# A 3×3 convolution with 2×2 max pooling: five row differences change engine, and the order of the head is rewritten

## The chip, the cores and the metric

The kernel runs on one core of a Trainium2 chip. The metric is the device time of one execution in microseconds (us), and where a kernel was run several times, the median. Engines are named as in the profile: PE is TensorE (PEld its weight loads), DVE is VectorE, ACT is ScalarE, POOL is GpSimd, and SP is SyncE, which here only issues DMA transfers.

## The reference

`x` has shape (16, 64, 64, 64), `weight` (128, 64, 3, 3), both float32. Each image is convolved with padding 1, and the maximum over 2×2 blocks is taken:

```python
conv[b, co] += weight[co, ci, kh, kw] * x_pad[b, ci, kh:kh+h, kw:kw+w]   # over ci, kh, kw
output[b, c, i, j] = np.max(conv[b, c, 2*i:2*i+2, 2*j:2*j+2])
```

The output has shape (16, 128, 32, 32).

## The kernel before

**Tiling.** Two images lie on the 128 partitions (two times 64 channels). The eight pairs of images are worked on as four groups `j`, each with one pair of the kind "k" and one of the kind "w". A pair is cut into four chunks `q` of 16 rows, which give 8 rows of pooled output. One chunk of a k pair and the same chunk of the w pair make a step `i` = 4j + q, so there are 16 steps.

**Arithmetic.** The two conv rows that a pooled row needs share input rows, so the kernel forms products with sums and differences of weight rows. For a k pair the weights alone are combined, and the rows of `x` go in as they are, plus the row sum `ks`. For a w pair the rows of `x` are combined as well, into four tiles: `ws` (sum of the two rows, step WS), `we` (their difference, step E), `wz` and `wy` (differences with the rows above and below, steps Z and Y). These read float32 rows from `wx` and write bfloat16 tiles for TensorE. `ks` reads and writes bfloat16. All of them pass through one function, `row_op` (line 248).

**Steps on TensorE** (`taps`, line 183): each group is six matmuls, three column taps for each of the two images. Step i has PA (two groups: 12 matmuls), PB (two), PR (uses KS) for the k pair, and P2 (uses E), P0 (uses Z), P3 (uses Y), P1 (uses WS) for the w pair: nine groups. A name such as PB.5 means PB of step 5.

**Accumulators.** There are four PSUM tiles `acc`, handed out from a queue `free` in the order in which the program text gives them back. PA and PB each take one for the k pair, P2 and SE (the seed, ScalarE) each one for the w pair.

**Steps that empty them.** EV (k) and ev (w) copy the first accumulator to SBUF on ScalarE (line 286) and free it. MX and mx take the maximum of the second accumulator and that copy on VectorE (line 299). PR.i adds after MX.i, and P1.i after mx.i. OD and od copy the odd columns on ScalarE (line 304), and CM and cm take the column maximum on VectorE (line 318), free the second accumulator and issue the output's DMA on SP. After CM.i the rows `wx` of step i + 4 are loaded, also on SP. SE.i writes minus the first accumulator to the second on ScalarE (line 295), ahead of P0.i.

**Order.** Nothing is reordered by the compiler: every engine works its queue in the order in which the program emits it. This order is written out by hand in three strings: `HEAD` (the weights, and steps 0 to 3), `STEADY` (run for i = 4 to 12, each name with an offset to i) and `TAIL`. `XO` and `XE` cast the first chunk of the first k pair on VectorE, X1 and X2 the second chunk on ScalarE, and the rest of that pair is loaded by `kload`, a DMA issued on POOL's queue that converts to bfloat16.

**VectorE and GpSimd.** Each GpSimd row operation waits for the last SBUF row operation that was emitted for VectorE ahead of it (`on_gpsimd`, `behind`): in `STEADY`, E, Z and Y of step i + 1 wait for WS.i. Before the change E.0, all KS and all WS are on VectorE, and E.1 to E.15, all Z and all Y on GpSimd. In the old `HEAD` some KS and WS come between E, Z and Y of a step. `kload` of the rest of the first pair is issued behind Y.0.

Of the kernel before, what the change touches and what calls it, by code (L numbers as in the profile page):

```python
# [11 lines left out]
def kernel(  # L12
# [21 lines left out]
    nc = tc.nc  # L34
# [4 lines left out]
    SUB = mybir.AluOpType.subtract  # L39

    B, CI, H, W = x.shape
# [28 lines left out]
    def behind(inst, other):  # L70
        if other is not None:
            tc.add_manual_dep(inst.ins, other.ins.name, SYNC, reason="order")

    def on_vector(inst):
        sbuf_op[0] = inst
        return inst

    def on_gpsimd(inst):
        behind(inst, sbuf_op[0])
        return inst  # L80


    def rows_of(p, lo, hi):
        return x[2 * p : 2 * p + 2].rearrange("b c h w -> (b c) h w")[:, lo:hi, :]

    def chunk(q):
        return (2 * R * q + (q > 0), min(H, 2 * R * (q + 1) + 1))
# [4 lines left out]
    def kload(j, lo, hi):  # L92
        if j not in kx:
            kx[j] = kx_pool.tile([128, H, W], BF16, name="kx")
        return nc.gpsimd.dma_start(out=kx[j][:, lo:hi, :], in_=rows_of(2 * j, lo, hi))  # L95
# [138 lines left out]
    def row_out(name, i):  # L234
        j, q = divmod(i, NQ)
        if (name, j) not in row:
            row[name, j] = row_pool.tile([128, HO, W], BF16, name=name)
        return row[name, j][:, q * R : (q + 1) * R, :]

    def row_in(t, first, pad):  # L240
        a = first + pad
        return t[:, a : a + 2 * R - 1 : 2, :]

    def row_op(engine, name, i, a, b, op):
        j, q = divmod(i, NQ)
        t, pad = (kx[j], 0) if name == "ks" else (wx[j % 2], 1)
        f = 2 * R * q
        return engine.tensor_tensor(  # L248
            out=row_out(name, i), in0=row_in(t, f + a, pad), in1=row_in(t, f + b, pad), op=op
        )  # L250
# [5 lines left out]
        on_vector(row_op(nc.vector, "ws", i, 0, 1, ADD))  # L256

    def we(i):
        if i == 0:
            on_vector(row_op(nc.vector, "we", i, 1, 0, SUB))  # L260
        else:
            on_gpsimd(row_op(nc.gpsimd, "we", i, 1, 0, SUB))

# [3 lines left out]
    def wy(i):  # L267
        on_gpsimd(row_op(nc.gpsimd, "wy", i, 2, 0, SUB))
        j, q = divmod(i, NQ)
        if i == 0:  # L270
            kload(0, chunk(2)[0], H)
        if q == 1 and j + 1 < NP // 2:
            kload(j + 1, 0, H // 2 + 1)
        if q == 2 and j + 1 < NP // 2:
            kload(j + 1, H // 2 + 1, H)


    ev, od, ot = {}, {}, {}
# [64 lines left out]
    def cast_more(first):  # L343
# [18 lines left out]
        "X2": lambda: cast_more(1),  # L362
        "PA": pa, "PB": pb, "PR": pr, "P0": p0, "P1": p1, "P2": p2, "P3": p3,
        "KS": ks, "WS": ws, "E": we, "Z": wz, "Y": wy, "SE": seed,
        "EV": lambda i, h=None: evac(("k", i), h), "ev": lambda i, h=None: evac(("w", i), h),
        "MX": lambda i, h=None: rowmax(("k", i), h), "mx": lambda i, h=None: rowmax(("w", i), h),
# [3 lines left out]
    for m in BLOCKS:  # L370
# [2 lines left out]

    HEAD = """
        D2 g0 D0 g2 GS g1 TD2 VD2 TG0 VG0 XO TD0 VD0 TG2 VG2 TG1 VG1 XE GM PA.0 GP TGM VGM TGP
        KS.0 E.0 WS.0 PB.0 EV.0 X1 Z.0 Y.0 VGP P2.0 MX.0 SE.0 X2 PA.1 EV.1 PR.0 P0.0 P3.0 E.1 P2.1 KS.1
        OD.0 CM.0 PB.1 Z.1 ev.0 WS.2 SE.1 P0.1 ev.1 mx.0 P1.0 od.0 Y.1 P3.1 MX.1 PR.1 OD.1 PA.2
        E.2 WS.1 KS.2 cm.0 PB.2 CM.1 P2.2 Z.2 mx.1 P1.1 EV.2 MX.2 PR.2 SE.2 od.1 cm.1 OD.2 CM.2
        Y.2 E.3 Z.3 Y.3 P0.2 P3.2 KS.3 WS.3 PA.3 E.4 ev.2 mx.2 P2.3 EV.3 Z.4 PB.3 SE.3 Y.4 MX.3
        P1.2 od.2 cm.2 P0.3 P3.3 ev.3 PR.3 KS.4 WS.4  # L380
    """
    STEADY = """
        PA+0 OD-1 E+1 CM-1 P2+0 mx-1 EV+0 Z+1 PB+0 SE+0 Y+1 P1-1 MX+0 P0+0 od-1 P3+0 cm-1 ev+0
# [63 lines left out]
```

## Time and profile before

| | us |
|---|---|
| median of 6 runs | 109.58 |
| lowest and highest | 108.97 and 110.64 |
| the profiled execution's own time | 110.64 |
| its span, first to last instruction | 108.8 |
| busy: PE, DVE, ACT, POOL | 100.7, 83.5, 72.9, 64.9 |

The profiled execution is the slowest of the six. The span leaves out what lies ahead of the first and behind the last instruction, here 1.8 us. A line of a timeline reads: start, duration (both us), engine, source line, operation, output and inputs with partitions × elements and type, and how many instructions are merged. In brackets stands the idle time ahead of it and what ended that. A line of the chain of waits reads: start, duration, engine, tile and source line. [...]

### The profile page before, as it was taken

How to read it: one execution, taken by the hardware profiler on the slowest of the kernel's cores; microseconds unless marked ns; L12 is line 12 of the kernel's file. 1: busy time of each engine (PE TensorE's matmuls, PEld its weight loads, DVE VectorE, ACT ScalarE, POOL GpSimd, SP SyncE). 2: the span in 40 equal slices, each digit the busy share in tenths (PEclk: the TensorE clock that was granted, in tenths of full speed). 3: DMA queues.
4: the chain of work that ended last, by engine and by line, in shares of the span. 5: the costliest groups of instructions: out<-in, count | busy, mean ns of one | idle time of the engine just before them, and what ended most of it. 6: DMA issues, size and time to landing. Idle time of an engine off the chain costs nothing.

```text
span 108.8 us, 2348 instructions
## 1 busy us (share of the span) xinstructions
PE 100.7 (93%) x900; PEld 52.1 (48%) x900; DVE 83.5 (77%) x109; ACT 72.9 (67%) x92; POOL 64.9 (60%) x73
## 2 busy tenths in 40 slices
PE   5999879999999999999999999999999999999820
PEld 2564434544545555555555555555555555545400
DVE  0494779996989786868797869688787888685950
ACT  4565966549666767676877876776867676776820
POOL 6200997699696969490869594943967444445000
PEclk9999999999999999999999999999999999999985
DMA  3999469999995979999974889999939422223052
GB/s 73 355 325 353 169 76 225 272 240 217 185 343 206 220 115 198 312 195 349 289 243 132 179 115 267 243 257 335 279 146 216 158 101 99 96 96 102 0 193 96
DMA packets 12475, 21.96 MB, mean 202 GB/s; under 512 B 944, under 2 KB 9136, under 8 KB 12464
## 3 DMA queue, kind: packets, MB, share of 16 engines
q1 hardware_dynamic: 11312, 18.03, 49.9%
q0 software_dynamic: 1008, 3.65, 22.8%
q8 instruction: 7, 0.11, 0.5%
q10 hardware_dynamic: 144, 0.13, 0.3%
q14 instruction: 4, 0.03, 0.1%
HBM read 17.07 MB, written 8.39 MB: 234 GB/s over the span
## 4 chain that ended last, share of the span: by engine, by line
PE 69%; DVE 14%; DMA 7%; issue 4%; ACT 2%; SPq 0%; DVEq 0%; ACTq 0%
PE acc L183 67%; DVE acc L299 9%; DMA ksecond<-in_x_dram 7%; DVE ws L248 2%; DVE o L318 2%; PE acc L135 2%; ACT od L304 2%; ACT kx L344 1%; DVE ks L248 0%; SPq L100 0%; DVE zeros L112 0%; DVEq L299 0%; ACTq L304 0%
## 5 line engine op out<-in xcount | busy, mean ns | idle before, releaser
L183 PEld LDWEIGHTS <-wt 64*128 64x128 bf16 x864 | 48.5, 94 | 47.6 <-issue 4.2
L299 DVE TENSOR_TENSOR acc<-acc,ev 128x1024 f32<-128x1024 f32 (+1 forms) x34 | 39.3, 1164 | 10.1 <-PE acc L183 9.4
L183 PE MATMUL acc<-kx,wt 64*128 64x504 bf16 (+3 forms) x384 | 46.6, 373 | 0.5 <-ACT kx L344 0.4
L286 ACT COPY ev<-acc 128x1024 f32<-128x1024 f32 (+1 forms) x34 | 32.6, 964 | 12.8 <-PE acc L183 11.2
L248 POOL TENSOR_TENSOR we<-wx 128x512 bf16<-128x512 f32 x15 | 19.1, 1273 | 17.3 <-DVE ws L248 9.3
L304 ACT COPY od<-acc 128x512 f32<-128x512 f32 x32 | 18.8, 587 | 11.3 <-PE acc L183 11.2
L318 DVE TENSOR_TENSOR o<-acc,od 128x512 f32<-128x512 f32 x32 | 21.8, 689 | 5.5 <-ACT od L304 5.5
L248 POOL TENSOR_TENSOR wz<-wx 128x512 bf16<-128x512 f32 x16 | 20.3, 1271 | 8.6 <-DVE ws L248 7.7
L248 POOL TENSOR_TENSOR wy<-wx 128x512 bf16<-128x512 f32 x16 | 20.3, 1270 | 5.6 <-DVE ws L248 5.6
L295 ACT ACTIVATE acc<-acc 128x1024 f32<-128x1024 f32 x16 | 16.1, 1008 | 2.6 <-PE acc L183 2.2
L183 PE MATMUL acc<-we,wt 64*128 64x504 bf16 (+1 forms) x96 | 13.3, 377 | 0.8 <-POOL we L248 0.5
L183 PE MATMUL acc<-ws,wt 64*128 64x504 bf16 (+1 forms) x96 | 13.3, 377 | 0.6 <-DVE acc L299 0.4
L183 PE MATMUL acc<-ks,wt 64*128 64x504 bf16 (+1 forms) x96 | 13.3, 377 | 0.2
L183 PE MATMUL acc<-wy,wt 64*128 64x504 bf16 (+1 forms) x96 | 13.3, 377 | 0.0
L183 PE MATMUL acc<-wz,wt 64*128 64x504 bf16 (+1 forms) x96 | 13.3, 377 | 0.0
L248 DVE TENSOR_TENSOR ws<-wx 128x512 bf16<-128x512 f32 x16 | 13.1, 821 | 0.0
L248 DVE TENSOR_TENSOR ks<-kx 128x512 bf16<-128x512 bf16 x16 | 8.9, 559 | 0.6 <-ACT kx L344 0.6
L135 PE MATMUL acc<-zeros 128*128 128x512 bf16 x8 | 3.6, 631 | 1.2 <-DVE zeros L112 1.2
L95 POOL DMA_DIRECT2D kx<-in_x_dram x7 | 4.1, 588 | 0.0
L148 PEld LDWEIGHTS <-wq 128*128 128x128 bf16 x28 | 2.6, 134 | 1.0 <-issue 0.6
L148 PE MATMUL acc<-ident,wq 128*128 128x128 bf16 x28 | 2.8, 281 | 0.0
L350 DVE TENSOR_TENSOR wq<-wraw 128x192 bf16<-128x192 f32 x1 | 0.5, 501 | 2.5 <-DMA wraw<-in_weight_dram 2.5
(26 smaller groups left out, 15.1 us busy)
## 6 DMA issues: line engine op xcount, KB each, us to landing
out_dram<-o SPq DMA_DIRECT2D x31, 256.0 KB, 4.3
wx<-in_x_dram SPq DMA_DIRECT2D x8, 512.0 KB, 7.4
wx<-in_x_dram SPq DMA_DIRECT2D x4, 544.0 KB, 8.8
kx<-in_x_dram POOLq DMA_DIRECT2D x4, 496.0 KB, 9.2
wx<-in_x_dram SPq DMA_DIRECT2D x4, 480.0 KB, 5.0
kx<-in_x_dram POOLq DMA_DIRECT2D x3, 528.0 KB, 8.9
kfirst<-in_x_dram SPq DMA_DIRECT2D x1, 544.0 KB, 4.2
ksecond<-in_x_dram SPq DMA_DIRECT2D x1, 512.0 KB, 7.4
```

What stands on the lines that cost most here:

```text
L95: return nc.gpsimd.dma_start(out=kx[j][:, lo:hi, :], in_=rows_of(2 * j, lo, hi))
L135: return nc.tensor.matmul(acc[t][:, h], zeros[:, 0:128], zeros, start=True, stop=True, skip_group_check=True)
L148: nc.tensor.transpose(tp[:, (j - lo) * 128 : (j - lo + 1) * 128], wq[:, j : j + 2, :].rearrange("a b c -> a (b c)"), ident,)
L183: nc.tensor.matmul(dst[:, half, i0:i1, o0:o1], wt[lo : lo + CI, m0 + kw - half, :], rows(lo, i0, i1, c0, c1), start=start and kw == 1, sto ...
L248: return engine.tensor_tensor(out=row_out(name, i), in0=row_in(t, f + a, pad), in1=row_in(t, f + b, pad), op=op)
L286: nc.scalar.copy(out=ev[g][:, halves(h)], in_=acc[ta[g]][:, halves(h)])
L295: nc.scalar.mul(acc[t], acc[ta["w", i]], -1.0)
L299: nc.vector.tensor_tensor(out=t, in0=t, in1=ev[g][:, halves(h)], op=MAX)
L304: nc.scalar.copy(out=od[g][:, halves(h)], in_=acc[tb[g]][:, halves(h), :, 1::2])
L318: nc.vector.tensor_tensor(out=o, in0=acc[tb[g]][:, s, :, 0::2], in1=od[g][:, s], op=MAX)
L344: nc.scalar.copy(out=kx[0][:, klo2 + first : khi2 : 2, :], in_=ksecond[:, first::2, :])
L350: "D2": lambda: on_vector(nc.vector.tensor_sub(out=slots(D2), in0=g2, in1=g1)),
```

## The change

Three things are changed.

1. E.1 to E.4 are computed on VectorE, where E.0 already was. E.5 to E.15 stay on GpSimd.
2. The load of the rest of the first k pair is issued on POOL's queue behind E.0, ahead of Z.0. Before, it was issued behind Y.0.
3. `HEAD` is reordered. In steps 1 to 4 WS, KS and E of a step stand together ahead of Z and Y, so that both GpSimd operations wait for the last of the three. Z.4 and Y.4, which stood ahead of KS.4 and WS.4, now stand behind them. The order of TensorE's groups, of the emptying steps and of the accumulators handed out changes somewhat. `STEADY` and `TAIL` are the same.

```diff
     def we(i):
-        if i == 0:
-            on_vector(row_op(nc.vector, "we", i, 1, 0, SUB))
+        if i < 5:
+            inst = on_vector(row_op(nc.vector, "we", i, 1, 0, SUB))
+            if i == 0:
+                behind(kload(0, chunk(2)[0], H), inst)
         else:
             on_gpsimd(row_op(nc.gpsimd, "we", i, 1, 0, SUB))
...
         j, q = divmod(i, NQ)
-        if i == 0:
-            kload(0, chunk(2)[0], H)
         if q == 1 and j + 1 < NP // 2:
...
-        KS.0 E.0 WS.0 PB.0 EV.0 X1 Z.0 Y.0 VGP P2.0 MX.0 SE.0 X2 PA.1 EV.1 PR.0 P0.0 P3.0 E.1 P2.1 KS.1
-        OD.0 CM.0 PB.1 Z.1 ev.0 WS.2 SE.1 P0.1 ev.1 mx.0 P1.0 od.0 Y.1 P3.1 MX.1 PR.1 OD.1 PA.2
-        E.2 WS.1 KS.2 cm.0 PB.2 CM.1 P2.2 Z.2 mx.1 P1.1 EV.2 MX.2 PR.2 SE.2 od.1 cm.1 OD.2 CM.2
-        Y.2 E.3 Z.3 Y.3 P0.2 P3.2 KS.3 WS.3 PA.3 E.4 ev.2 mx.2 P2.3 EV.3 Z.4 PB.3 SE.3 Y.4 MX.3
-        P1.2 od.2 cm.2 P0.3 P3.3 ev.3 PR.3 KS.4 WS.4
+        KS.0 E.0 WS.0 PB.0 EV.0 X1 Z.0 Y.0 VGP P2.0 MX.0 SE.0 X2 PA.1 EV.1 WS.1 KS.1 E.1 PR.0
+        P0.0 P3.0 Z.1 Y.1 OD.0 CM.0 P2.1 ev.0 PB.1 SE.1 mx.0 P0.1 P1.0 MX.1 P3.1 ev.1 od.0 PR.1
+        WS.2 KS.2 E.2 Z.2 Y.2 OD.1 cm.0 CM.1 PA.2 EV.2 P2.2 PB.2 SE.2 mx.1 P1.1 P0.2 MX.2 P3.2
+        od.1 ev.2 cm.1 E.3 KS.3 WS.3 Z.3 Y.3 PR.2 PA.3 OD.2 CM.2 P2.3 mx.2 EV.3 PB.3 SE.3 P1.2
+        MX.3 P0.3 od.2 P3.3 cm.2 ev.3 PR.3 E.4 KS.4 WS.4 Z.4 Y.4
```

## The prediction

> **What bounds the kernel now.** I read the engine shares of the page first, then the chain of waits in order of time, then each engine's timeline from 10 to 46 us.
>
> ```profile
> PE 100.7 (93%) x900; PEld 52.1 (48%) x900; DVE 83.5 (77%) x109; ACT 72.9 (67%) x92; POOL 64.9 (60%) x73
> ```
> ```profile
> 30.22 63.98 PE acc L183 x594
> ```
>
> The second line, from the chain, decides: from 30.22 to 94.19 us the end is set by TensorE alone, with no wait of another engine in between. A change in the head helps only if it brings this run forward, and only as far as nothing inside the run is then late. One group of six matmuls follows the next every 0.65 us and a step has nine, so a step is 5.84 us (PA.4 at 32.81, PA.6 at 44.40). PA.4 starts at 32.81 us; from PA.1 at 11.54 to there lie 30 groups, 19.4 us of work in 21.3 us. So 1.8 us lie open in the head's TensorE queue, and no more can be won there. Now the head's DVE and POOL queues:
>
> ```profile
> 14.58 0.69 DVE L318 TENSOR_TENSOR o<-acc,od 128x512 f32<-128x512 f32 x1 [0.80 <-ACT od L304]
> 15.19 2.04 DVE L248 TENSOR_TENSOR ws<-wx 128x512 bf16<-128x512 f32 x1
> 17.15 2.35 DVE L299 TENSOR_TENSOR acc<-acc,ev 128x1024 f32<-128x1024 f32 x2
> 19.42 1.53 DVE L248 TENSOR_TENSOR ws<-wx 128x512 bf16<-128x512 f32 x1
> ...
> 26.90 1.52 DVE L248 TENSOR_TENSOR ks<-kx 128x512 bf16<-128x512 bf16 x1
> ```
> ```profile
> 14.16 1.29 POOL L248 TENSOR_TENSOR we<-wx 128x512 bf16<-128x512 f32 x1
> 15.40 1.27 POOL L248 TENSOR_TENSOR wz<-wx 128x512 bf16<-128x512 f32 x1
> 17.31 1.27 POOL L248 TENSOR_TENSOR wy<-wx 128x512 bf16<-128x512 f32 x1 [0.64 <-DVE ws L248]
> ```
>
> A row sum `ws` takes 0.68 us alone (that of 28.34 us does), `ks` 0.42. Here they take 2.04, 1.53 and 1.52, and end 0.56, 0.56 and 0.30 us after the GpSimd row operation beside them. The one at 15.19 was queued during E.1 and waited through Z.1 too: back-to-back GpSimd operations did not let VectorE in. The row maximum (`acc<-acc,ev`), with one input in PSUM, keeps its 1.2 us beside GpSimd. Last, the steady part, where the change's wake arrives:
>
> ```profile
> 33.80 1.28 POOL L248 TENSOR_TENSOR we<-wx 128x512 bf16<-128x512 f32 x1 [0.96 <-DVE ws L248]
> 35.03 1.27 POOL L248 TENSOR_TENSOR wz<-wx 128x512 bf16<-128x512 f32 x1
> 36.26 1.27 POOL L248 TENSOR_TENSOR wy<-wx 128x512 bf16<-128x512 f32 x1
> ```
> ```profile
> 38.06 0.42 DVE L248 TENSOR_TENSOR ks<-kx 128x512 bf16<-128x512 bf16 x1
> 38.39 0.68 DVE L248 TENSOR_TENSOR ws<-wx 128x512 bf16<-128x512 f32 x1
> 39.40 0.69 DVE L318 TENSOR_TENSOR o<-acc,od 128x512 f32<-128x512 f32 x1 [0.32 <-ACT od L304]
> ```
>
> GpSimd's step-5 block ends at 37.53 and KS.5 starts at 38.06: the two miss each other by half a microsecond. The column maximum CM.4 ends at 40.09, and PB.5, which reuses its accumulator, starts at 40.51: 0.4 us of slack.
>
> [...] E.0 on VectorE took 693 (0.61 from start to start in a queue).
>
> **The change, part by part.** E.1 to E.4 leave GpSimd (4 × 1.27 us) and add 4 × 0.61 = 2.4 us to VectorE. `kload` of the rest of the first image pair moves from behind Y.0 (issued 13.44, landed 6.1 us later) to behind E.0, ahead of Z.0. I walk the new queues with durations and gaps of the old trace: a group of six ends 0.83 after its start, an engine reacts in 0.03 to 0.08 us, GpSimd operations start 1.23 apart.
>
> - *To step 1.* Unchanged up to E.0 (ends 10.26). The load's issue takes 0.70, so Z.0 starts at 11.04 instead of 11.00 and Y.0 ends at 13.54. It lands near 17 to 19, before PA.2 at 19.65 needs it. Behind the waiting issue stand only Z.0 and Y.0; P0.0 (13.48) and P3.0 (14.13) have 0.6 us or more. WS.1 arrives at 12.3 and blocks to 13.54, ends 14.10; KS.1 and E.1 end at 14.45 and 15.05. P2.1 starts at 15.11 (before: 15.51). The rows for WS.1 landed at 12.34; the earlier load may delay that by 1.2 us at no cost.
> - *Steps 1 to 3.* CM.0 now stands behind E.1 and ends at 15.66; PB.1 wants its accumulator at 15.76. SE.1 ends at 16.98, P0.1 wants it at 17.06; ev.2 at 25.41, PA.3 wants it at 25.49. CM.2 ends 27.23 for PB.3 at 27.44. All others have 0.2 us or more: Z.1 starts behind E.1, Y.1 ends 17.63 for P3.1 at 18.36; WS.2, KS.2, E.2 run 18.43 to 20.06 with GpSimd idle; E.3, KS.3, WS.3 25.00 to 26.62, likewise. So TensorE runs through from 15.11: 25 groups × 0.648 = 16.2, and PA.4 starts at 31.33. That is **1.48 us earlier** than 32.81. If the three tight places slip by 0.05 each, 0.15 goes; I take that.
> - *The wake.* E.4, KS.4, WS.4 follow cm.2 (starts 30.23) and end at 32.46. Z.4 and Y.4 wait for WS.4; in the old order they preceded it. Behind them stand E.5, Z.5, Y.5, which wait for nothing more. GpSimd thus runs five operations in one piece: 32.54 + 4 × 1.23 + 1.27 = 38.73. KS.5 is due where it was relative to PA.4 (38.06 − 32.81 = 5.25): at 36.58. It is blocked for 2.15 us, to 38.73, and ends at 39.02; WS.5 at 39.63; CM.4 at 40.24; PB.5 starts at 40.28. Undelayed it would have started at 40.51 − 1.48 = 39.03. So 1.25 of the 1.48 us are given back, and 0.23 us stay before the slip. Should GpSimd yield once between two operations, KS.5 passes and WS.5 is caught behind Y.5 instead, with the same end to 0.2 us. The waiting KS.5 holds WS.5, CM.4, mx.4; only CM.4 is wanted early (mx.4 ends by 41.4, P1.4 wants it at 41.6).
> - *Later steps.* E.6 starts at 39.7 (before: 39.17) and Y.6 ends at 43.45; KS.6 is due at 43.7. The collision does not repeat. What has the same order from here on takes the same time.
>
> Sum: −1.48 + 1.25 + 0.15 = −0.08 us against the profiled execution's 110.64 (span 108.8). That execution is the longest of the six; the difference is applied to the median: 109.58 − 0.08 = **109.5 us**.
>
> **Unknown costs.** The slip lies between 0 (the walk holds) and 0.6 (each tight place by 0.2). [...] The block at KS.5 costs from 0 (VectorE runs KS.5 and WS.5 in one go between two GpSimd operations) to 1.25. The load of step 8's rows, the longest in the trace (issued 40.58, 11.5 us to landing), holds E.8:
>
> ```profile
> 52.23 1.27 POOL L248 TENSOR_TENSOR we<-wx 128x512 bf16<-128x512 f32 x1 [3.50 <-DMA wx<-in_x_dram]
> ...
> 55.48 0.77 DVE L248 TENSOR_TENSOR ks<-kx 128x512 bf16<-128x512 bf16 x1
> ```
>
> KS.8 is already held by 0.35 us there; CM.7 has 0.3 us left. Its issue comes after CM.4, 0.15 us later than now, while the `kx` load issued at 37.47 moves to 38.7: between 0 and 1.5 us of delay at landing; I take none beyond the slack.
>
> **Rivals.**
> - *A, faster: the block at KS.5 is not there.* GpSimd's block is broken long enough for KS.5 and WS.5 together. Then most of the 1.48 us stays: 109.58 − 1.48 + 0.15 = 108.25, say 108.3. [...] Against it: the 2.04 us row sum.
> - *B, slower: the load for E.8 lands later.* Place: step 8. A landing later by d shifts E.8 to Y.8 by d, KS.8 waits as long, and PB.8 by d − 0.3: it decides from d = 0.3. With d = 1.5, as far as the neighbouring `kx` load moves, the cost is 1.2: 110.7. For it: DMA is busy over 95% from 40 to 55 us, and E.8 has no spare time. Against it: the requests of the head all come earlier, so the backlog at 40 us should be no larger.
> - *C, the head's tight places all slip (0.6 us).* WS.4 and GpSimd's block move along, so nothing hides it: 109.9, within 1%.
>
> **How the numbers follow.** About 1% is what a measurement of this kernel tells from no change (its six runs span 1.5%). Forecast 0.45, C 0.15, A 0.22, B 0.18. Forecast and C are both within 1%: 0.60; A gives faster by over 1%, 0.22; B slower, 0.18. The range runs from A's 108.3 to B's 110.7. The likeliest case alone: 109.2 to 109.9.
>
> **What would show it.** In the changed profile: P2.1 near 15.1; row sums in the head at their bare 0.4 and 0.7 us except WS.1 (1.8 us); PA.4 near 31.3 to 31.5; five GpSimd row operations in one piece from about 32.5; KS.5 lasting about 2.4 us; TensorE idle for about 1.2 us ahead of PB.5, which starts near 40.4. It is wrong if KS.5 takes 0.4 us (A), if the gap is at PB.8 (B), or if PA.4 starts after 32 us because one of the walk's margins was no margin.

## The result, and the profile after

Over all runs the kernel before takes 109.46 us (median of 72) and the changed kernel 108.96 us (median of 35). The ratio is 0.9955, with a 95% interval of 0.994 to 0.997: half a microsecond faster, within 1%. Medians here and below are over all executions, while ratios leave out those over 1.5% longer than the fastest of the same kernel, so the two can differ. The profiled execution of the changed kernel took 108.92 us, with a span of 107.1.

The spans, 108.8 and 107.1, differ by 1.7 us, over three times the change in the medians. Most of the difference arises ahead of the change. In the first profile of the kernel before, the rows for E.0 came late: E.0 started at 9.57 us (8.01 in the changed kernel's profile), and PA.1 at 11.54 (10.38). So I count from PA.1 below. Each kernel was also profiled a second time (experiment 8), and both profiles are given. "The last group" is the last group of matmuls, P1.15.

| us | before, two profiles | changed, two profiles | predicted |
|---|---|---|---|
| PA.1 to P2.1 | 3.97, 3.64 | 3.42, 3.69 | 3.57 |
| PA.1 to PA.4 | 21.27, 21.36 | 19.61, 19.87 | 19.79 |
| PA.4 to PB.5 | 7.70, 7.70 | 8.82, 8.82 | 8.95 |
| PA.1 to PB.5 | 28.97, 29.06 | 28.43, 28.69 | 28.74 |
| PA.1 to the last group | 91.65, 92.16 | 91.12, 91.61 | |

The starts of PA.1, PA.4 and PB.5 in the first profiles, first of the kernel before, then of the changed kernel (PB.5 of the latter stands further down):

```profile
11.54 1.47 PE L183 MATMUL acc<-kx,wt 64*128 64x512 bf16 x12 [0.39 <-ACT kx L344]
...
32.81 1.40 PE L183 MATMUL acc<-kx,wt 64*128 64x512 bf16 x12
...
40.51 1.48 PE L183 MATMUL acc<-kx,wt 64*128 64x512 bf16 x12
```
```profile
10.38 1.47 PE L183 MATMUL acc<-kx,wt 64*128 64x512 bf16 x12
...
29.99 1.40 PE L183 MATMUL acc<-kx,wt 64*128 64x512 bf16 x12
```

Next the chain of waits of the changed kernel, from its longest run of TensorE on (start, duration, what):

```profile
13.80 20.19 PE acc L183 x186
...
35.24 1.24 DVE ks L248
36.48 1.68 DVE ws L248
38.16 0.61 DVE o L318
...
38.81 53.68 PE acc L183 x498
```

From P2.1 (13.80) on TensorE alone sets the end, 16.4 us earlier than before (30.22). But the chain leaves TensorE at 34 us: TensorE works on until 37.9 us and then stands still, and what it waits for is KS.5, WS.5 and CM.4. GpSimd's timeline shows why, then VectorE's and TensorE's:

```profile
31.23 1.27 POOL L248 TENSOR_TENSOR wz<-wx 128x512 bf16<-128x512 f32 x1 [3.30 <-issue]
32.47 1.27 POOL L248 TENSOR_TENSOR wy<-wx 128x512 bf16<-128x512 f32 x1
33.69 1.28 POOL L248 TENSOR_TENSOR we<-wx 128x512 bf16<-128x512 f32 x1
34.92 1.28 POOL L248 TENSOR_TENSOR wz<-wx 128x512 bf16<-128x512 f32 x1
36.15 1.46 POOL L248 TENSOR_TENSOR wy<-wx 128x512 bf16<-128x512 f32 x1
```
```profile
35.24 1.24 DVE L248 TENSOR_TENSOR ks<-kx 128x512 bf16<-128x512 bf16 x1
36.40 1.75 DVE L248 TENSOR_TENSOR ws<-wx 128x512 bf16<-128x512 f32 x1
38.08 0.68 DVE L318 TENSOR_TENSOR o<-acc,od 128x512 f32<-128x512 f32 x1
```
```profile
38.81 1.47 PE L183 MATMUL acc<-kx,wt 64*128 64x512 bf16 x12 [0.94 <-DVE o L318]
```

The five operations Z.4, Y.4, E.5, Z.5, Y.5 stand in one piece. KS.5 comes at 35.24, during Z.5, takes 1.24 us instead of 0.42, and ends 0.28 us after Z.5. Y.5, beside KS.5 and WS.5, takes 1.46 instead of 1.27 us, and WS.5 takes 1.75 instead of 0.68 and ends 0.54 us after Y.5. CM.4 is late, and PB.5 with it. The 0.94 us in brackets count from the end of the group ahead, but groups start 0.65 us apart, last 0.83 and so overlap by 0.18 us, so PB.5 comes 1.12 us later than it could have. In the head the row operations take their bare times (0.68 us for E.1; the 693 that the prediction gives for E.0 are ns):

```profile
11.62 1.19 DVE L248 TENSOR_TENSOR ws<-wx 128x512 bf16<-128x512 f32 x1 [0.37 <-DMA wx<-in_x_dram]
12.73 0.41 DVE L248 TENSOR_TENSOR ks<-kx 128x512 bf16<-128x512 bf16 x1
13.06 0.68 DVE L248 TENSOR_TENSOR we<-wx 128x512 bf16<-128x512 f32 x1
```

Only WS.1 is held, beside Y.0 (10.98 to 12.25 us), as foreseen: it takes 1.19 us here, less than the foreseen 1.8, since it had to wait for its rows first, and 1.93 us in the second profile. The early load left little to spare. It took 9.0 us to land here, 0.4 us ahead of the start of PA.2 (18.39), and KS.2 waited for it; in the second profile PA.2 (18.03) did not wait either. KS.2 here:

```profile
18.02 0.43 DVE L248 TENSOR_TENSOR ks<-kx 128x512 bf16<-128x512 bf16 x1 [0.23 <-DMA kx<-in_x_dram]
```

### The profile page after: what moved, and what is told of

The parts are those of the page before. It is cut to its first block, busy times and chain, and to the rows that moved or that the text cites. A ratio compares the mean times of both kernels' runs of the same rounds, so it can differ in the third digit from the quotient of the medians.

```text
span 107.1 us, 2346 instructions
## 1 busy us (share of the span) xinstructions
PE 99.7 (93%) x900; PEld 51.6 (48%) x900; DVE 84.0 (78%) x113; ACT 72.8 (68%) x92; POOL 60.2 (56%) x69
## 3 DMA queue, kind: packets, MB, share of 16 engines
q1 hardware_dynamic: 11312, 18.03, 51.1%
## 4 chain that ended last, share of the span: by engine, by line
PE 85%; DVE 9%; issue 1%; ACT 1%; DVEq 0%
PE acc L183 79%; DVE acc L299 5%; PE acc L135 3%; PE acc L148 2%; DVE ws L248 2%; DVE o L318 1%; DVE ks L248 1%; ACT od L304 1%; DVE zeros L112 0%; DVEq L299 0%
## 5 line engine op out<-in xcount | busy, mean ns | idle before, releaser
L183 PEld LDWEIGHTS <-wt 64*128 64x128 bf16 x864 | 48.1, 94 | 46.5 <-issue 2.3
L183 PE MATMUL acc<-kx,wt 64*128 64x504 bf16 (+3 forms) x384 | 46.6, 373 | 0.9 <-DVE o L318 0.9
L286 ACT COPY ev<-acc 128x1024 f32<-128x1024 f32 (+1 forms) x34 | 32.5, 964 | 12.5 <-PE acc L183 10.9
L248 POOL TENSOR_TENSOR we<-wx 128x512 bf16<-128x512 f32 x11 | 14.0, 1273 | 13.5 <-DVE ws L248 9.3
L183 PE MATMUL acc<-ws,wt 64*128 64x504 bf16 (+1 forms) x96 | 13.2, 377 | 0.4 <-DVE acc L299 0.4
L183 PE MATMUL acc<-ks,wt 64*128 64x504 bf16 (+1 forms) x96 | 13.2, 377 | 0.1
L183 PE MATMUL acc<-wz,wt 64*128 64x504 bf16 (+1 forms) x96 | 13.3, 377 | 0.0
L183 PE MATMUL acc<-wy,wt 64*128 64x504 bf16 (+1 forms) x96 | 13.2, 377 | 0.0
L183 PE MATMUL acc<-we,wt 64*128 64x504 bf16 (+1 forms) x96 | 13.2, 377 | 0.0
L248 DVE TENSOR_TENSOR ws<-wx 128x512 bf16<-128x512 f32 x16 | 12.5, 783 | 0.4 <-DMA wx<-in_x_dram 0.4
L248 DVE TENSOR_TENSOR ks<-kx 128x512 bf16<-128x512 bf16 x16 | 7.5, 468 | 0.2 <-DMA kx<-in_x_dram 0.2
L248 DVE TENSOR_TENSOR we<-wx 128x512 bf16<-128x512 f32 x5 | 3.4, 683 | 0.0
```

The lines of the kernel that those rows point to most:

```text
L183: nc.tensor.matmul(dst[:, half, i0:i1, o0:o1], wt[lo : lo + CI, m0 + kw - half, :], rows(lo, i0, i1, c0, c1), start=start and kw == 1, sto ...
L248: return engine.tensor_tensor(out=row_out(name, i), in0=row_in(t, f + a, pad), in1=row_in(t, f + b, pad), op=op)
L286: nc.scalar.copy(out=ev[g][:, halves(h)], in_=acc[ta[g]][:, halves(h)])
```

## The experiments

Ratios are to the kernel before, with 95% intervals.

**1. Z.4 behind Y.3.** If GpSimd's piece costs the microsecond, one operation moved out of it, into GpSimd's idle stretch, should bring it back.

```diff
-        od.1 ev.2 cm.1 E.3 KS.3 WS.3 Z.3 Y.3 PR.2 PA.3 OD.2 CM.2 P2.3 mx.2 EV.3 PB.3 SE.3 P1.2
-        MX.3 P0.3 od.2 P3.3 cm.2 ev.3 PR.3 E.4 KS.4 WS.4 Z.4 Y.4
+        od.1 ev.2 cm.1 E.3 KS.3 WS.3 Z.3 Y.3 Z.4 PR.2 PA.3 OD.2 CM.2 P2.3 mx.2 EV.3 PB.3 SE.3 P1.2
+        MX.3 P0.3 od.2 P3.3 cm.2 ev.3 PR.3 E.4 KS.4 WS.4 Y.4
```

> The changed kernel with one edit: Z.4 stands behind Y.3 instead of behind WS.4, so GpSimd does it in its idle stretch (27.9 to 31.2 us in the changed profile). Theory (the gain of the head is given back because GpSimd runs five operations in one piece behind WS.4 [...]): the piece is four operations, ends 1.23 us earlier, about when KS.5 is due; KS.5 is held by Y.5 alone (about 1.2 us in all), WS.5 takes its bare 0.68, PB.5 has no gap. About 1.0 us faster than the changed kernel, 1.4 to 1.6 us faster than the kernel before, ratio about 0.986. Rival (PB.5 waits for something else, such as its output's transfer or ScalarE): time as the changed kernel, ratio about 0.995, and the gap of 0.9 us ahead of PB.5 stays.

Measured: 108.13 us, ratio 0.990 (0.986 to 0.994). The gap ahead of PB.5 is gone: PA.5 starts at 35.77 and PB.5 at 37.72, with no idle time. WS.5 takes its bare time on VectorE:

```profile
35.27 1.19 DVE L248 TENSOR_TENSOR ks<-kx 128x512 bf16<-128x512 bf16 x1
36.39 0.68 DVE L248 TENSOR_TENSOR ws<-wx 128x512 bf16<-128x512 f32 x1
```

The theory stands and its rival falls. The gain over the changed kernel is smaller than the 1.0 us that was expected: 0.83 us on the medians, 0.6 by the ratios. The same timelines, GpSimd's first, show a new break at step 12:

```profile
73.62 1.27 POOL L248 TENSOR_TENSOR we<-wx 128x512 bf16<-128x512 f32 x1 [4.50 <-DMA wx<-in_x_dram]
```
```profile
76.33 1.75 DVE L248 TENSOR_TENSOR ws<-wx 128x512 bf16<-128x512 f32 x1
```
```profile
78.74 1.48 PE L183 MATMUL acc<-kx,wt 64*128 64x512 bf16 x12 [0.32 <-DVE o L318]
```

The last line is PB.12, which was due at 78.24, 0.65 us after P2.12, and is 0.50 us late. E.12 waits for its rows, issued at 61.0 us and landing after 12.5. GpSimd's block comes late and stands on KS.12 and WS.12, which take 0.53 and 1.75 us (0.42 and 0.68 at step 11).

**2. Rows loaded earlier.** On top of experiment 1, the rows of step i + 5 are loaded behind cm.i.

```diff
-        if g[0] == "k" and g[1] + NQ < N and h is None:
-            wload(g[1] + NQ)
+        if g == ("k", 0):
+            wload(NQ)
+        if g[0] == "w" and g[1] + NQ + 1 < N and h is None:
+            wload(g[1] + NQ + 1)
```

> The kernel with Z.4 behind Y.3, and with the rows of step i + 5 loaded behind cm.i instead of behind CM.(i+1), about 1.9 us earlier in each step. Theory (with the head's gain kept, the next limit is the load for E.12, which landed at 73.6 us and moved GpSimd's block onto KS.12): E.12 starts up to 1.9 us earlier, WS.12 takes its bare 0.68 us, no gap ahead of PB.12: 0.3 to 0.5 us faster than with Z.4 alone, ratio to the kernel before 0.985 to 0.989. Rival (the transfers are limited by throughput, so that an earlier request lands no earlier, or holds up a kx load): ratio 0.990 or more.

Measured: 107.77 us, ratio 0.985 (0.982 to 0.988). Run once more:

> The kernel with Z.4 behind Y.3 and the row loads one step part earlier, once more, for its interval and a profile with an earlier first load. Theory: ratio to the kernel before 0.983 to 0.988, TensorE without a gap over 0.2 us from P2.1 to P0.13, last group 90.0 to 90.4 us after PA.1. Rival (its advantage over Z.4 alone was chance): 0.989 or more.

Measured: 107.59 us, ratio 0.980 (0.975 to 0.984), a little better than expected. In its profile the rows for E.12 are asked for at 59.2 us and land after 6.6. E.12 starts at 71.54 and waits for WS.11, not for its rows (in the profile of the first run likewise, at 72.90). The chain of waits of this second run shows the whole middle as one piece:

```profile
14.01 77.56 PE acc L184 x720
```

The last group starts 90.27 us after PA.1 (changed kernel: 91.12 and 91.61). This version beats both kernels.

**3. E.5 on VectorE as well.** A second way to take one operation out of the piece: `if i < 6` in `we`.

> The changed kernel with E.5 on VectorE too. Theory (a piece of five operations behind WS.4 costs 1.1 us at PB.5): the piece is Z.4, Y.4, Z.5, Y.5, four operations; E.5 costs VectorE 0.6 us ahead of CM.3, for which PB.4 has 0.15 us to spare, so PB.4 starts 0.45 us later and PB.5 then waits 0.3 to 0.6 instead of 1.1. In all 0.0 to 0.5 us faster than the changed kernel, ratio to the kernel before 0.990 to 0.996. Rival (GpSimd's piece is not the cause): 0.45 us slower than the changed kernel, ratio 0.999 or more.

Measured: 108.52 us, ratio 0.990 (0.987 to 0.994). The gap at PB.5 is gone here too, where 0.3 to 0.6 us had been expected to stay. PB.4 waits 0.33 us for CM.3 instead (idle before it in TensorE's timeline), which stands behind E.5, and PB.12 waits 0.64 us, as in experiment 1. In this execution, the longest of the six with 109.1 us, these two waits use up what the gap had cost. Over all executions, two different ways of shortening the piece give the same ratio.

**4. The load back behind Y.0**, all else as in the changed kernel.

```diff
-            inst = on_vector(row_op(nc.vector, "we", i, 1, 0, SUB))
-            if i == 0:
-                behind(kload(0, chunk(2)[0], H), inst)
+            on_vector(row_op(nc.vector, "we", i, 1, 0, SUB))
...
+        if i == 0:
+            kload(0, chunk(2)[0], H)
```

> The changed kernel with the load of the rest of the first k pair back behind Y.0. Theory (the earlier load is needed because the new head reaches PA.2 a microsecond sooner): the issue comes about 3 us later; KS.2 or PA.2 waits for the load, PA.4 and with it the whole rest come 0.5 to 1.5 us later, ratio to the kernel before between 1.000 and 1.010. Rival (the earlier load does nothing, since the load took 6.1 us in the kernel before and would land in time): as the changed kernel, ratio 0.995 within 0.002.

Measured: 109.35 us, ratio 0.998 (0.995 to 1.001). This lies between the theory's range (1.000 to 1.010) and the rival's (0.993 to 0.997), and the interval reaches into both, so it decides for neither. The profiled execution shows the wait that the theory names, PA.2 waiting for the load, which is issued at 11.82 us and takes 8.0 us to land:

```profile
19.88 1.47 PE L183 MATMUL acc<-kx,wt 64*128 64x512 bf16 x12 [1.60 <-DMA kx<-in_x_dram]
```

So the late load can cost 1.6 us here; this execution, 110.78 us, was among the longest of its kernel. The executions spread from 108.35 to 111.25 us, those of the changed kernel only from 108.45 to 109.85. That the late load makes the long ones is shown for this one execution alone. By the ratios the loss against the changed kernel is about 0.3%, with overlapping intervals.

**5. Only the load moved**, in the kernel before.

```diff
     def we(i):
         if i == 0:
-            on_vector(row_op(nc.vector, "we", i, 1, 0, SUB))
+            inst = on_vector(row_op(nc.vector, "we", i, 1, 0, SUB))
+            behind(kload(0, chunk(2)[0], H), inst)
...
-        if i == 0:
-            kload(0, chunk(2)[0], H)
```

> The kernel before with only the load of the rest of the first k pair moved behind E.0. Theory (the old head reaches PA.2 about when the late load lands, so the early load alone takes away a wait only in some executions): ratio to the kernel before 0.997 to 1.001. Rival (the early load is most of the gain of the change): 0.995 or less. Second rival (the early load holds up the loads that the head waits for, E.0's and WS.1's rows): 1.003 or more.

Measured: 109.03 us, ratio 0.997 (0.995 to 0.9995). This is a gain, at the edge of what the theory allowed, and for a reason that it did not have. GpSimd's timeline has E.1 right behind Y.0, since the load's issue (0.70 us) no longer lies between them:

```profile
10.95 1.27 POOL L248 TENSOR_TENSOR wy<-wx 128x512 bf16<-128x512 f32 x1
12.18 1.26 POOL L248 TENSOR_TENSOR we<-wx 128x512 bf16<-128x512 f32 x1
```

P2.1 starts 3.25 us after PA.1 (before: 3.97 and 3.64), PA.4 20.74 (21.27 and 21.36), and the last group 91.13, as early as in the changed kernel (91.12 and 91.61). PA.2 did not wait for the load in either profile of the kernel before.

**6. Only the engine changed**: the kernel before with `if i < 5` in `we`, old order and old load.

> The kernel before, in its old order and with its old load, with E.1 to E.4 on VectorE. Theory: part of the head's gain comes (P2.1 0.3 to 0.6 us earlier), the old interleaving keeps row sums waiting beside Z and Y, and there is no piece of five operations, since Z.4 and Y.4 stand ahead of KS.4 and WS.4. Ratio to the kernel before 0.994 to 0.998. Rival (order is everything): 1.000 within 0.002. Second rival (the added VectorE work delays the maxima in the old order): 1.003 or more.

Measured: 112.27 us, ratio 1.014 (1.005 to 1.022). The six executions spread from 110.15 to 115.28 us, and the ratio rests on the two shortest. My theory failed; the second rival held. VectorE's timeline has WS.3 and E.4 held beside Z.3 and Y.3 (1.76 and 1.75 us instead of 0.68), ahead of mx.2, and in TensorE's timeline P1.2 waits for mx.2:

```profile
26.43 1.76 DVE L248 TENSOR_TENSOR ws<-wx 128x512 bf16<-128x512 f32 x1
28.12 1.75 DVE L248 TENSOR_TENSOR we<-wx 128x512 bf16<-128x512 f32 x1
```
```profile
31.06 0.82 PE L183 MATMUL acc<-ws,wt 64*128 64x512 bf16 x6 [2.39 <-DVE acc L299]
```

PA.2 waits for the load as well, 0.91 us. I had counted the five-operation piece as the only danger and had not walked the old order with the added operations.

**7. Order and load, without the engine**: the changed kernel with `if i == 0` in `we`.

> The changed kernel with E.1 to E.4 back on GpSimd, in the new order of the head. Theory (the new order needs the fast E): E.1 on GpSimd starts behind KS.1 and ends 0.7 us later than on VectorE, P2.1 likewise; E.4 delays P2.4, and behind WS.4 GpSimd has six operations in one piece. 1.5 to 2.5 us slower than the changed kernel, ratio to the kernel before 1.009 to 1.018. Rival (the order alone carries the gain and the engine of E is indifferent): ratio 0.995 within 0.003.

Measured: 109.25 us, ratio 0.999 (0.997 to 1.002). My expectation failed: the loss against the changed kernel is about 0.4 us, not 1.5 to 2.5. The rival's ratio, 0.995 within 0.003, was not met either, though the intervals overlap. I had placed E.4 behind WS.4. In the program it stands ahead of KS.4, waits for WS.3 only, and runs at 27.95 us in GpSimd's idle stretch, so the piece has five operations as in the changed kernel, not six. P2.1 is late as foreseen:

```profile
14.48 0.83 PE L183 MATMUL acc<-we,wt 64*128 64x512 bf16 x6 [0.83 <-POOL we L248]
```

But the 0.6 to 0.8 us by which PA.4 is later (20.42 after PA.1) vanish at PB.5, which waits 0.36 us where the changed kernel waits 0.94 and comes 28.64 us after PA.1 (28.43 and 28.69). What this profile still loses it loses at PB.12, which is 0.38 us late, as in experiment 1.

**8. Both kernels profiled again.**

> The kernel before once more, for a second profile. The first had E.0 at 9.57 us, the kernels since then near 8.0. Theory (the late start of that execution is a late first load and nothing of the kernel): E.0 near 8.0 to 8.3, PA.1 near 10.3, P2.1 3.97 us after PA.1 as before, PE's last group 91.3 to 92.0 us after PA.1, span near 107.6. Open: whether PA.2, then due near 19.2, waits for the late load (issued near 12.2, 6 to 8 us to landing): 0 to 1 us. Rival (a late E.0 belongs to the kernel before): E.0 again above 9 us.

> The changed kernel once more, for a second profile. Theory (the give-back is fixed by GpSimd's piece of five): PA.4 19.6 us after PA.1 within 0.2, PB.5 7.6 to 7.8 us after the end of WS.4, a gap of 0.9 to 1.2 us ahead of PB.5. Rival (the gap was an accident of one execution, for example of a load): no gap, or one elsewhere.

Measured: the kernel before has E.0 at 8.00 us and PA.1 at 10.28, and takes 109.85 us; the late start in the first profile was that execution's. PA.2 does not wait for the load. P2.1 comes 3.64 us after PA.1, not 3.97 as in the first profile. The last group comes 92.16 us after PA.1, a little over what was expected, and the span is 108.1 instead of 107.6: PB.12 is 0.42 us late, behind a KS.12 of 1.53 us. The changed kernel takes 108.78 us; PB.5 waits again (both programs have one line more at the top, so L183 is L184):

```profile
38.44 1.47 PE L184 MATMUL acc<-kx,wt 64*128 64x512 bf16 x12 [0.95 <-DVE o L319]
```

From the end of WS.4 to the start of PB.5 there are 7.71 us in the first profile (31.10 to 38.81), 7.71 in the second (30.73 to 38.44), 7.72 with the load back (32.94 to 40.66) and 7.72 without the engine (31.16 to 38.88), though these four reach WS.4 at times that differ by 2.2 us. The piece sets PB.5.

## Why the prediction was right

**The head.** PA.4 was to come 1.48 us earlier; it came 1.66 and 1.49 us earlier in pairs of first and second profiles. From P2.1 to PA.4 TensorE ran through in 16.19 and 16.18 us, predicted 16.2. Of the three tight places (PB.1, P0.1, PA.3) none slipped by more than 0.04 us, and PB.3 made up for that: the PB of a pair's last chunk takes 1.21 us, where I had counted 1.30. So the 0.15 us that I took off were too much, and rival C is out. How the gain divides was less certain than its size. P2.1 was to come 0.40 us earlier; in the first pair it came 0.55 us earlier, in the second 0.05 us later, and there the whole gain lies between P2.1 and PA.4 (17.72 us before, 16.18 changed). That the early load did not hold up PA.2 was foreseen, but with 0.4 us to spare in one profile it owes something to luck.

**The give-back.** PB.5 was to come 7.82 us after WS.4's end; it came 7.71. PA.4 to PB.5 grew by 1.12 us, predicted 1.25. Experiments 1 and 3 show the cause. The account of how VectorE is held was only half right: KS.5 took 1.24 us, not the 2.4 us that I named as a sign. I read from one row sum (2.04 us) that back-to-back GpSimd operations do not let VectorE in. Here KS.5 came in between Z.5 and Y.5: it ended 0.28 us after Z.5, although Y.5 started at 36.15, before Z.5 had ended. WS.5 was caught behind Y.5 (1.75 us). That is the alternative which the prediction priced as "the same end to 0.2 us", and so it was. How long a held operation has to wait was my estimate from three held durations (2.04, 1.53 and 1.52 us); a rule for it is not shown, there or here. Rival A, which needed VectorE to pass twice, is out.

**The later steps.** The collision did not repeat at KS.6 (0.41 us). Rival B is out at its place: E.8 (49.18) waited for WS.7 (to 49.04) and not for its load. The mechanism exists, though, at E.12, where the prediction did not look for it. In the profile of experiment 1 the rows land late (after 12.5 us), GpSimd's block moves onto KS.12 and WS.12, and PB.12 is 0.50 us late. It is also late by 0.42 us in the second profile of the kernel before, behind the KS.12 of 1.53 us, and by 0.24 in the second of the changed kernel. In the two first profiles PB.12 is on time.

**The sum.** Predicted −0.08 us, measured −0.50 on the medians. The direction and the two large terms held; mis-sized were the small ones that are left when these are subtracted. The slip (0.15 us) was none. The give-back was 0.13 us smaller. Together this gives −0.36, and PA.1 to PB.5 differs by −0.54 and −0.37 in the two pairs; up to the last group it is −0.53 and −0.55, the second with 0.18 us from PB.12. What is left is less than the two profiles of one kernel differ by at the last group (0.5 us). The 109.2 to 109.9 us that I gave for the likeliest case alone were missed from below; 0.12 us of that is the kernel before, 109.46 us over all its executions and not the 109.58 of the first six. Any sum between about −1.1 and +1.1 us would have been within 1%, so it is the times of PA.4 and PB.5 that bear the mechanism out, and not the total.

**What the parts are worth.** The prediction priced the load's move only by when it lands and by what it delays. It left out what the move takes away: 0.70 us of GpSimd's queue ahead of E.1. For the whole change that is no omission, since E.1 is not on GpSimd there, but the worth of the load's move alone turns on it. In the kernel before, this alone is worth 0.3% (experiment 5), and all three edits together 0.45%, with overlapping intervals: that the other two edits add anything to it is not shown. Alone, E on VectorE loses 1.4% or more, and order with load gains nothing that can be told from zero. The edits are not additive: the faster head of the full change is mostly spent at PB.5.

## What to carry to other kernels

Work that is moved behind a wait can come out as one piece with what is queued behind it, here five GpSimd operations from 31.23 to 37.61 us; look one step further for the operations of another engine that fall due beside that piece, here KS.5 and WS.5 (1.24 and 1.75 us instead of 0.42 and 0.68). A head faster by 1.5 us was worth 0.5 here, and one operation moved out of the piece brought some 0.6 us more (ratio 0.990 against 0.9955). When two large terms nearly cancel, the forecast's error is that of the small ones, so walk each queue as emitted, with every operation and every DMA issue in it: the two expectations that failed outright (6 and 7) came from a queue that was not walked.

## What was not expected of the hardware

- A VectorE row operation beside back-to-back GpSimd operations was not always held to the end of both: KS.5 in the changed kernel (1.24 us) entered between two of them. In the first profile of the kernel before, a row sum was passed over once (2.04 us, through E.1 and Z.1). In the second, KS.1 took 2.04 us beside a load's issue (0.70 us) and E.1 (1.29). What decides who is next stays open.
- The same load lands at very different times: the rows for E.0 after 3.9 us (experiment 4) to 6.4 (first profile of the kernel before), the rest of the first k pair after 6.1 us there and 9.0 in the first profile of the changed kernel. From experiment 1 to the second run of experiment 2, E.12's rows were asked for 1.8 us sooner and landed 7.7 us sooner (6.6 instead of 12.5 us to landing). The earlier request is not all of it: in the first profile of the changed kernel they were asked for at 62.1 us, 1.1 us later than in experiment 1, and took 10.8 us to land, 1.7 less. What makes this load long in some executions stays open.
